# Short-convolution projections as 2x2x2 blocks in seven products, mixer outputs through DRAM scratch, two gates moved behind the last scan

## The chip, the core and the metric

One core of one Trainium2 chip runs the whole step. TensorE (PE, with its weight loads shown as PEld), VectorE (DVE), ScalarE (ACT), GpSimd (POOL) and the DMA queues work side by side, each in its own order; SyncE (SP) issues all transfers of this kernel. The metric is the device time of one execution in microseconds (us): three runs of the kernel before gave 1789.61, 1789.62 and 1792.41, median 1789.62.

## The reference

One layer of a hybrid decoder on 1088 tokens (1024 of a prompt, 64 of eight samples), width 1024, float32:

```python
h = rmsnorm(x, g_mix_pre) * (1 + scale_m) + shift_m
proj = h @ w_in                       # 1024 -> 3*1024 (B, C, x) + 1024 (z) + 2048 (xbc) + 16 (dt)
sc_b, sc_c, sc_x, z, xbc, dt_raw = jnp.split(proj, idx, axis=-1)
u = sc_c * sc_x
uc, new_sc_buf = causal_dwconv(u, sc_buf, sc_conv_w)
y_sc = sc_b * uc
xbc_c = silu(causal_dwconv(xbc, ...))                 # x, B, C of the scan, 4 groups
y_ssd, new_state = ssd_scan(xs, dt, A, Bm, Cm, d_skip, ssm_state)
yg = (y_ssd * silu(z)).reshape(bsz, L, SSM_GROUPS, SSM_WIDTH // SSM_GROUPS)
y_ssd = rmsnorm(yg, 1.0).reshape(bsz, L, SSM_WIDTH) * ssm_norm_g
mix = jnp.concatenate([y_sc, y_ssd], axis=-1) @ w_out
x = x + gate_m * rmsnorm(mix, g_mix_post)
f = (silu(h2 @ w_gate) * (h2 @ w_up)) @ w_down        # h2: normed and modulated x
x = x + gate_f * rmsnorm(f, g_ffn_post)
```

The modulation vectors (shift, scale, gate) are six slices of silu(c) @ w_ada + b_ada. The outputs are x, the new convolution rows and the new scan states.

## The kernel before

Activations lie transposed: 128 channels on the partitions, 1088 tokens along the row. Every large product takes float32 operands as a high part `hi` (a cast on ACT) and a rest `lo` (a subtraction on DVE), and is three matmuls per 128 input channels: `hi*hi`, `hi*lo`, `lo*hi` (`acc3`, lines 335 to 340). The modulated input is held as eight pairs `hh[k]`, `hl[k]`.

A planner orders the instructions. It goes by program order, takes what is ready by its own estimate of times, and writes out one fixed order for each engine; a tile has a slot in a pool with a fixed number of buffers, and its first writer waits until a slot is free. `in_order` (line 1073) puts the PE instructions of a call behind the last PE instruction traced before it, and only those.

The stages, in order:

- the input norm, the modulation and the first projection (lines 94 to 567);
- four scan groups, `ssd(g)` (line 693). `merge` (line 955) interleaves its steps with a list `side` that gives PE other work: `group_tiles(g+1)` (the projections of the next group), from g=1 on `gate(g-1)` (line 892: six projection tiles of z, silu, multiply) and `norm(g-1)` (line 903: squares, column sums on PE, a chain of small DVE operations for the inverse root, `rsqrt_of`, line 263, its spread over the partitions on PE, `spread`, line 276, and the scaling), and at g=3 `short_conv(0)`;
- `gate(3)`, then `short_conv(1)` to `short_conv(3)` (line 914), into which `norm(3)` and the two later modulation products `ada_steps(1)`, `ada_steps(2)` (line 188) are merged. A call of `short_conv` covers 256 channels: C, x and B, each two output tiles of three token chunks (`CH`: 384, 384, 320 columns) with 24 matmuls; u = C*x, a convolution over three rows and the multiply by B follow on DVE;
- the output projection (lines 1042 to 1165): first the scan half, whose eight outputs are split into hi and lo from where they stand (lines 1057 to 1063), for all tokens; then the short-convolution half in three token chunks, split by `out_split` (line 1078), with the residual rows of the chunk before (`mix_tail`, line 1113) between its tiles;
- the feed-forward part (lines 1167 to the end). Its gate and up products are already 2x2x2 blocks in seven products: `combos_w` (line 1258) builds seven weight combinations from two raw halves, `sums_x` (line 1240) four sums of the input blocks, and `unit` (line 1313) runs the seven products in the order of `ORDER` (line 1174) for two token blocks `QS` of halves of 256 and 288 columns: 7 * 2 * 4 * 3 = 168 matmuls for 256 output channels, into PSUM banks A, C and B; after each product the running sum is copied (ACT) or added (DVE) to its output.

```python
    ORDER = ((1, "A", True, 0, 0, True), (5, "C", True, 1, 1, True), (6, "A", False, 0, 1, True),
             (3, "C", False, 0, 1, False), (7, "A", False, 1, 1, False), (2, "B", True, 0, 0, False),
             (4, "A", False, 1, 0, True))
```

(each entry: product, bank, whether the bank is new, output block, half, whether it is that output's first write)

The mixer's outputs stay on chip, most of them in the 18 buffers of the pool `fmp`, until the output projection has read them.

## Time and profile before

| what | us |
|---|---|
| median of three runs | 1789.62 |
| the profiled execution | 1787.29 |
| its span, first to last instruction | 1785.6 |
| PE busy in the span | 1715.8 |
| DVE busy in the span | 1066.7 |
| four scan groups (125 to 545 us of the span) | 420 |
| gate(3), short_conv(1..3), two modulation products (545 to 800) | 255 |
| output projection and residual (800 to 1060) | 260 |

The profile's page gives busy time per engine, the span in 40 slices, the DMA queues, the chain of work that ended last and the costliest groups. In a group's row stand the line, engine, operation, tiles (out<-in), shapes, count, then busy us and the mean ns of one, then the idle time of the engine just before them with what ended it. A matmul's mean is longer than its spacing, since matmuls overlap; the spacing is a stretch of time divided by the number of matmuls in it. The view of stretches gives, for each, its length, then busy us and instruction count of each engine, the granted PE clock, the DMA share and GB/s. The timeline gives start, duration, engine, line and operation, with runs of the same instruction merged.

### The profile page before, as it was taken

The numbers are of one execution on the slowest core, as the hardware profiler recorded it, in microseconds if no ns is written. First come the engines' busy times: TensorE is split into PE (matmuls) and PEld (weight loads), VectorE is DVE, ScalarE is ACT, GpSimd is POOL, SyncE is SP. The second block draws the span as 40 slices with busy tenths as digits, with TensorE's granted clock in tenths as the row PEclk, the third lists the DMA queues.
The fourth block names the chain that finished last, engine by engine and source line by source line (L and its number), as shares of the span: only waits on it lengthen the run. The fifth ranks groups of instructions, "written<-read, shape, count | busy, mean of one in ns | idle before, by whom it ended". The sixth has DMA issues, their size and how long they took to land.

```text
span 1785.6 us, 30704 instructions
## 1 busy us (share of the span) xinstructions
PE 1715.8 (96%) x12336; PEld 1629.9 (91%) x12336; DVE 1066.7 (60%) x2175; ACT 716.1 (40%) x1485; POOL 261.3 (15%) x361
## 2 busy tenths in 40 slices
PE   5999999999999999999999899999999999899997
PEld 4998999998889999999989799999999998899987
DVE  5588777876562413142047868666665676678845
ACT  3456563554312110113245765444444444422303
POOL 2111001010010001000040000022222200332303
PEclk8999999999999999999999899999999999999999
DMA  9210303021112144432134833433434448856243
GB/s 313 72 35 25 86 13 100 22 70 42 35 58 64 60 140 151 144 104 90 48 101 147 259 116 124 144 136 136 147 134 150 152 156 293 329 208 243 101 150 119
DMA packets 144885, 224.02 MB, mean 125 GB/s; under 512 B 9153, under 2 KB 118897, under 8 KB 142438
## 3 DMA queue, kind: packets, MB, share of 16 engines
q1 hardware_dynamic: 144742, 222.06, 36.7%
q8 instruction: 97, 1.59, 0.4%
q14 instruction: 46, 0.38, 0.1%
HBM read 168.48 MB, written 53.55 MB: 124 GB/s over the span
## 4 chain that ended last, share of the span: by engine, by line
PE 84%; DVE 6%; ACT 3%; DMA 3%; issue 2%; POOL 1%; SPq 1%; DVEq 0%; POOLq 0%; ACTq 0%
PE pm L338 15%; PE pm L340 15%; PE pm L339 15%; PE pz L1309 5%; PE pz L1311 5%; PE pz L1310 5%; PE pm L1309 4%; PE pm L1311 4%; PE pm L1310 4%; PE pm L197 1%; PE pz L755 1%; DMA raw<-in_w_up 1%; PE pz L760 1%; DMA raw<-in_w_in 1%; PE pz L749 1%
## 5 line engine op out<-in xcount | busy, mean ns | idle before, releaser
L340 PE MATMUL pm<-h,wl 128*128 128x384 f32 (+1 forms) x810 | 266.8, 329 | 0.0
L339 PE MATMUL pm<-h,wh 128*128 128x384 f32 (+1 forms) x810 | 266.7, 329 | 0.0
L338 PE MATMUL pm<-h,wh 128*128 128x384 f32 (+1 forms) x810 | 266.6, 329 | 0.0
L315 ACT CAST wh<-raw 128x512 fp32r<-128x512 f32 (+1 forms) x141 | 87.9, 651 | 312.3 <-PE pm L339 204.0
L316 DVE TENSOR_TENSOR wl<-raw,wh 128x512 fp32r<-128x512 f32 (+1 forms) x123 | 87.4, 726 | 146.6 <-ACT wh L315 143.1
L338 PEld LDWEIGHTS pm<-h,wh 128*128 128x128 f32 x810 | 153.0, 189 | 1.4 <-issue 1.0
L339 PEld LDWEIGHTS pm<-h,wh 128*128 128x128 f32 x810 | 152.9, 189 | 1.2 <-issue 0.7
L340 PEld LDWEIGHTS pm<-h,wl 128*128 128x128 f32 x810 | 152.9, 189 | 1.0 <-issue 0.9
L338 PE MATMUL pm<-bt,wh 128*128 128x384 f32 (+2 forms) x350 | 121.3, 347 | 0.5 <-ACT wh L315 0.5
L340 PE MATMUL pm<-bt,wl 128*128 128x384 f32 (+2 forms) x350 | 115.0, 329 | 0.2 <-DVE wl L316 0.2
L339 PE MATMUL pm<-bt,wh 128*128 128x384 f32 (+2 forms) x350 | 114.8, 328 | 0.0
L338 PEld LDWEIGHTS pm<-bt,wh 128*128 128x128 f32 x350 | 66.2, 189 | 18.4 <-issue 6.6
L432 DVE SCALAR_TENSOR_TENSOR fm<-ext,vT,fm 128x1024 f32<-128x1024 f32 x57 | 72.7, 1276 | 0.0
L1202 DVE TENSOR_TENSOR fs<-f,fs 128x512 fp32r<-128x512 f32 (+1 forms) x80 | 54.6, 695 | 26.9 <-ACT fs L1201 26.3
L339 PEld LDWEIGHTS pm<-bt,wh 128*128 128x128 f32 x350 | 66.4, 190 | 1.7 <-issue 0.3
L1201 ACT CAST fs<-f 128x512 fp32r<-128x512 f32 (+1 forms) x80 | 46.7, 598 | 52.7 <-DMA f_d<-fs 33.1
L340 PEld LDWEIGHTS pm<-bt,wl 128*128 128x128 f32 x350 | 66.3, 189 | 1.6 <-DVE wl L316 0.4
L1326 DVE TENSOR_TENSOR facc<-facc,pz 128x288 f32<-128x288 f32 x124 | 55.9, 451 | 15.8 <-PE pz L1311 15.5
L1326 DVE TENSOR_TENSOR facc<-facc,pm 128x256 f32<-128x256 f32 x124 | 51.5, 415 | 5.7 <-PE pm L1311 5.2
L1273 POOL TENSOR_TENSOR raw<-raw 128x512 f32<-128x512 f32 x16 | 22.1, 1378 | 206.4 <-DVE raw L1271 206.4
L338 PE MATMUL pm<-fm,wh 128*128 128x512 f32 (+2 forms) x144 | 46.6, 325 | 0.0
L340 PE MATMUL pm<-fm,wl 128*128 128x304 f32 (+2 forms) x144 | 46.6, 325 | 0.0
(4655 smaller groups left out, 5338.1 us busy)
## 6 DMA issues: line engine op xcount, KB each, us to landing
raw<-in_w_in SPq DMA_DIRECT2D x48, 512.0 KB
fc<-f_d SPq DMA_DIRECT2D x9, 2016.0 KB
f_d<-fs SPq DMA_DIRECT2D x31, 576.0 KB
wa<-in_w_ada SPq DMA_DIRECT2D x32, 512.0 KB
raw<-in_w_out SPq DMA_DIRECT2D x32, 512.0 KB
fc<-f_d SPq DMA_DIRECT2D x9, 1792.0 KB
f_d<-fs SPq DMA_DIRECT2D x31, 512.0 KB
raw<-in_w_gate SPq DMA_DIRECT2D x28, 512.0 KB
```

Source lines behind the costliest of these rows:

```text
L315: (nc.gpsimd.tensor_copy if hi_eng else nc.scalar.copy)(wh, raw)
L316: (eng or nc.vector).tensor_tensor(wl, raw, wh, op=sub)
L338: mm(ps[:, :n], wh, xh, start=(first and j == 0), stop=False)
L339: mm(ps[:, :n], wh, xl, start=False, stop=False)
L340: mm(ps[:, :n], wl, xh, start=False, stop=(last and j == end))
L432: nc.vector.scalar_tensor_tensor(po, e[:, j:j + NP], taps[j], po, op0=mult, op1=add)
L1201: nc.scalar.copy(hi, v)
L1202: (eng or nc.vector).tensor_tensor(lo, v, hi, op=sub)
L1309: mm(ps, W[0][k], X[0][k], start=(start and k == 0), stop=False, skip_group_check=True)
L1310: mm(ps, W[0][k], X[1][k], start=False, stop=False, skip_group_check=True)
L1311: mm(ps, W[1][k], X[0][k], start=False, stop=(stop and k == nk - 1), skip_group_check=True)
L1326: nc.vector.tensor_tensor(out(q, i, h), out(q, i, h), ps, op=add)
```

## The change

- **Short convolution.** The C, x and B projections of each 256 channels become three `unit`s (the function of the feed-forward part, with a new argument for the token blocks, here `SQ`: four halves of 272 columns). Their input blocks are `hh`/`hl` themselves for products 1 and 2, and sums of blocks for 5, 6, 4 (`sums_h`, into new tiles) and for 7 and 3; the sum for 7 is written over the second halves of `hh[0..3]`, `hl[0..3]` (`sums_last`), after the last plain projection has read them. All four channel groups now run after the last scan.
- **Order.** `ada_steps(1)` and `ada_steps(2)` move into the `side` of scan groups 1 and 2; `gate(0)`, `norm(0)` and `gate(1)` are the `side` of group 3; gates 2 and 3 run after it as `gate_late`, with the steps of `sums_h` and the first steps of `norm(1)` between their tiles; the rest of the norms 1, 2 and 3 is put between the products of the first two units (`late`), and what is left of them then runs ahead of the third.
- **norm.** It gets more steps (13), one chain of small operations for all nine token columns in place of three, the addition of squares on DVE in place of POOL, and ends by splitting its result and storing both parts in DRAM (`y_out`, scratch `y_d`). Its temporaries come from `new()`: a pool of one buffer (`psx`) for groups 1 to 3.
- **Outputs.** The short convolution's results are split and stored in the same way; the output projection loads hi and lo from `y_d` in both halves, and the splits there go.
- **gate.** silu is taken in place in PSUM (no `gz` tile).
- **Pools.** The scan groups' x tiles 2 to 7 lie in `yp2` (2 buffers) and `yp4` (4), which the units later use for C or x, for u (`e`) and for B (`cb`); `fmp` has 8 buffers. The feed-forward part is unchanged; its helpers stand earlier in the file.

```diff
+SQ = [(0, 272), (544, 272)]
...
+    h2p = pool(mid, "h2p", 4)
+    yp4, yp2 = pool(mid, "yp4", 4), pool(mid, "yp2", 2)
...
-        out = fm()
+        out = yt(yp2 if ct < 4 else yp4) if 1 < ct < 8 else fm()
...
+    def norm(g, y, new):
+        ps = pz()
+        sq = []
+        def sums(c):
+            for j in range(3):
+                mm(ps[:, 3 * c + j:3 * c + j + 1], sq[c][:, 0, j * P:(j + 1) * P], ones[:, 0:1],
+                   start=(c == 0 and j == 0), stop=(c == 2 and j == 2))
+        for c, (c0, n) in enumerate(CH):
+            q = new()[:, :768].rearrange("p (m n) -> p m n", m=2)
+            sq.append(q)
...
+            for m in range(2):
+                nc.scalar.square(q[:, m, :n], y[m][:, c0:c0 + n])
+            nc.vector.tensor_tensor(q[:, 0, :n], q[:, 0, :n], q[:, 1, :n], op=add)
+            yield
+            yield
+            sums(c)
+        r = rsqrt_of(ps[:, 0:9], 2 * P)
+        yield
+        yield
         for c, (c0, n) in enumerate(CH):
-            rs = spread(token_rstd(y, c), n)
+            rs = spread(r[:, 3 * c:3 * c + 3], n)
             for m in range(2):
                 v = y[m][:, c0:c0 + n]
                 nc.vector.scalar_tensor_tensor(v, v, sng[:, 2 * g + m:2 * g + m + 1], rs, op0=mult, op1=mult)
             yield
+        for m in range(2):
+            hi = new()[:, :T].bitcast(F32R)
+            lo = y[m].bitcast(F32R)
+            split(hi, lo, y[m])
+            y_out(8 + 2 * g + m, hi, lo)
+            yield
+
+    def y_out(k, hi, lo):
+        nc.sync.dma_start(y_d[k][:, 0], hi.bitcast(F32))
+        nc.sync.dma_start(y_d[k][:, 1], lo.bitcast(F32))
...
-        if g > 0:
-            side += [gate(g - 1, tl[g - 1][:2]), norm(g - 1, tl[g - 1][:2])]
+        side = [group_tiles(g + 1, tl[g + 1])] if g < 3 else []
+        if g in (1, 2):
+            side.append(ada_steps(g))
         if g == 3:
-            side.append(short_conv(0))
-        run(merge(ssd(g, *tl[g]), itertools.chain(*side), (0.67, 1.17, 1.17, 1.5)[g]))
-    ada = itertools.chain(ada_steps(1), ada_steps(2))
-    run(gate(3, tl[3][:2]))
-    run(merge(itertools.chain(short_conv(1), short_conv(2), short_conv(3)),
-              itertools.chain(norm(3, tl[3][:2]), ada), 0.4))
+            side += [gate(0, tl[0][:2]), norm(0, tl[0][:2], fm_row), gate(1, tl[1][:2])]
+        run(merge(ssd(g, *tl[g]), itertools.chain(*side), (0.67, 1.17, 1.17, 1.2)[g]))
...
+    left.close()
+    rws, wsc = pool(left, "rws", 4), pool(left, "wsc", 8)
+    x56, x4 = pool(left, "x56", 8), pool(left, "x4", 4)
+    pap, psx, psy = pool(left, "pap", 2), pool(left, "psx", 1), pool(left, "psy", 1)
...
+        vs_ = [pap, psx, pap]
+        for k in range(4):
+            v = [yt(in_turn(vs_)) for _ in range(2)]
+            for j in range(2):
+                nc.vector.tensor_tensor(v[j], hh[k + 4 * j], hl[k + 4 * j], op=add)
+            (b11, b12), (b21, b22) = blocks_h(v[0]), blocks_h(v[1])
+            nc.vector.tensor_tensor(b11, b12, b11, op=sub)
+            part(X_t[5][k][:, 0], X_t[5][k][:, 1], b11)
+            yield
...
+    def sums_last():
+        for k in range(4):
+            t = psy.tile([P, 2, 272], F32, tag="t3", name=nm("t3"))
...
+            nc.vector.tensor_tensor(t, b22l, b12l, op=sub)
+            nc.vector.tensor_tensor(t, t, b22h, op=add)
+            nc.vector.tensor_tensor(t, t, b12h, op=sub)
+            part(b12h, b12l, t)
...
+    sums = sums_h()
+    norm1, norm2, norm3 = (norm(g, ys[g], sx_row) for g in (1, 2, 3))
+    W2 = plain_w(w_in, 3072 + 512)
+    gate_late(2, ys[2], W2, {n: [sums, sums] for n in range(6)})
+    W3 = plain_w(w_in, 3072 + 768)
+    gate_late(3, ys[3], W3, {0: [norm1], 1: [norm1], 2: [norm1], 3: [norm1], 4: [norm1], 5: [norm1]})
+    run(sums)
+    sums_last()
...
+    late = [itertools.chain(norm1, norm2, norm3)]
+    pairs = [pap, yp2]
+    kept = []
+    for pr in range(4):
+        cc, cx = [[yt(pairs[(pr + j) % 2]) for _ in range(2)] for j in range(2)]
+        steps_ = {n: late for n in range(7)} if pr == 0 else {}
+        sc_unit(1024 + 256 * pr, cc, steps_)
+        sc_unit(2048 + 256 * pr, cx, steps_)
+        if pr == 0:
+            run(*late)
+        ext = []
+        for m in range(2):
...
+            e = yp4.tile([P, 1115], F32, tag="y", name=nm("y"))
...
+            conv(cc[m], e, es, [scw[:, j, ct:ct + 1] for j in range(3)], ct, None)
+            ext.append(e)
+        cb = [yt(yp4) for _ in range(2)]
+        sc_unit(256 * pr, cb, {})
+        for m in range(2):
+            y, hi, lo = cc[m], ext[m][:, :T].bitcast(F32R), cb[m].bitcast(F32R)
+            nc.vector.tensor_tensor(y, y, cb[m], op=mult)
+            split(hi, lo, y)
+            kept.append((2 * pr + m, hi, lo))
...
+    fa, fx, fb = pool(left, "fa", 4), pool(left, "fx", 8), pool(left, "fb", 7)
...
-    for k, y in enumerate(yall[8:]):
...
-        split(hi, lo, y)
+    for k in range(KT):
+        v = [(fx, btp, h2p)[(k > 3) + (k > 5)].tile([P, T], F32R, tag="bt" if k in (4, 5) else "fm", name=nm("hb"))
+             for _ in range(2)]
+        for e in range(2):
+            nc.sync.dma_start(v[e].bitcast(F32), y_d[8 + k][:, e])
...
-            split(*parts_, yall[k][:, c0:c0 + n])
+            nc.sync.dma_start(hb.bitcast(F32), y_d[k][:, :, c0:c0 + n])
...
-    out_proj(0, terms[0], {0: [nxt], 2: [nxt]}, lambda mp: out_load(mp, nc.gpsimd))
+    out_proj(0, terms[0], {0: [nxt], 2: [nxt]}, out_load)
```

`sc_unit` calls `unit` with the seven weight combinations of the given columns, all of them built on ACT and DVE; `late` is one list of one chain, so each product of the first two units takes one step of it.

More of the change, by code (lines that the diff above doesn't have):

```diff
@@ L141, in hymba_step @@
     load_first(1)
-    xt += [load_x(t, fmp, "fm") for t in range(3, 6)]
+    xt += [load_x(t, yp2 if t < 5 else yp4, "y") for t in range(3, 6)]
     wa0 += [load_quarter(q) for q in range(1, 4)]
@@ L146, in hymba_step @@
         hl.append(h_tile(k))
-    xt += [load_x(t, fmp, "fm") for t in range(6, 9)]
+    xt += [load_x(t, yp4, "y") for t in range(6, 9)]
     ident = const([P, P], "ident")
@@ new lines, in in_order, with in_turn, raw_half @@
+    def in_order(f, *a):
+        last = next(x for x in reversed(nc.cur_bb.bb.instructions) if x.engine == nc.tensor.engine)
+        with tc.issue_after(last):
+            return f(*a)
+    def in_turn(pools):
+        pools.append(pools.pop(0))
+        return pools[-1]
+    def raw_half(w, j, cols):
+        p = in_turn(raw_from)
+        raw = p.tile([P, 4, 256], F32, tag="bt" if p is btp else "wc", name=nm("raw"))
+        nc.sync.dma_start(raw, w[j * 512:(j + 1) * 512, cols:cols + 256].rearrange("(k p) n -> p k n", p=P))
+        return raw
@@ new lines, in plain_w, with product @@
+    def plain_w(w, cols):
+        raws = [raw_half(w, j, cols) for j in range(2)]
+        W = {}
+        for m in range(2):
+            for j in range(2):
+                t = in_turn(w_from).tile([P, 2, 4, P], F32R, tag="wc", name=nm("wp_"))
+                part(t[:, 0], t[:, 1], raws[j][:, :, m * P:(m + 1) * P])
+                W[m, j] = [[t[:, s, k] for k in range(4)] for s in range(2)]
+        return W
+    def product(ps, W, X, nk, start, stop):
+        for k in range(nk):
+            mm(ps, W[0][k], X[0][k], start=(start and k == 0), stop=False, skip_group_check=True)
+            mm(ps, W[0][k], X[1][k], start=False, stop=False, skip_group_check=True)
+            mm(ps, W[1][k], X[0][k], start=False, stop=(stop and k == nk - 1), skip_group_check=True)
@@ new lines, in unit @@
+    def unit(W, X, nk, qs, out, first=True, between={}, blocks_=QS):
+        B = {}
+        for n, (p, b, new, i, h, opens) in enumerate(ORDER):
+            for q in qs:
+                if new:
+                    B[b, q] = (pm, pz)[q]()
+                ps = B[b, q][:, :blocks_[q][1]]
+                in_order(product, ps, W[p], X[q][p], nk, new, p in (3, 2, 4))
+                if first and opens:
+                    nc.scalar.copy(out(q, i, h), ps)
+                else:
+                    nc.vector.tensor_tensor(out(q, i, h), out(q, i, h), ps, op=add)
+            for gen in between.get(n, ()):
+                in_order(next, gen, None)
@@ new lines, in sx_row, with sc_unit @@
+    def sx_row():
+        return yt(psx)
+    sums = sums_h()
[6 more added lines that the diff above has]
+    sums_last()
+    def sc_unit(cols, tiles, between):
+        unit(combos_w(w_in, cols, nc.vector), X_sc, 4, [0, 1],
+             lambda q, i, h: tiles[i][:, SQ[q][0] + 272 * h:SQ[q][0] + 272 * (h + 1)], True, between, SQ)
@@ L1149, in rows_fm @@
     def rows_fm():
[L1150 to L1152 removed]
+        return yt(yp4, (P, D))
+    G_m = post_rows(0, lambda: yt(yp2, (P, D)))
     terms = [out_split(0)]
```

266 lines of the change are left out of this document (108 added, 158 removed).

## The prediction

> **What bounds the kernel now.** I read the page first, for the busiest engine and the chain that ended last.
>
> ```profile
> span 1785.6 us, 30704 instructions
> PE 1715.8 (96%) x12336; PEld 1629.9 (91%) x12336; DVE 1066.7 (60%) x2175; ACT 716.1 (40%) x1485; POOL 261.3 (15%) x361
> PE 84%; DVE 6%; ACT 3%; DMA 3%; issue 2%; POOL 1%; SPq 1%; DVEq 0%; POOLq 0%; ACTq 0%
> ```
>
> PE is busy for 96% of the span and carries 84% of the chain. So a matmul less is time less, as long as nothing else becomes late. Then I read the view of stretches, one for each stage that the change touches.
>
> ```profile
> 552.00:572.00 20.00, 20.00 (x121) 20.00 (x120) 4.51 (x8) 6.51 (x15) 3.20 (x7) 1.00 0.16 53
> 1150.00:1450.00 300.00, 300.00 (x2391) 300.00 (x2390) 184.98 (x297) 141.64 (x284) 71.38 (x69) 1.00 0.40 142
> 125.00:205.00 80.00, 77.64 (x587) 68.92 (x586) 68.30 (x122) 48.80 (x105) 8.24 (x22) 1.00 0.25 69
> 409.00:545.00 136.00, 129.56 (x904) 121.28 (x903) 78.49 (x180) 43.32 (x101) 10.63 (x16) 0.97 0.17 50
> 545.00:800.00 255.00, 254.83 (x1574) 237.11 (x1573) 79.56 (x169) 36.82 (x71) 17.08 (x31) 1.00 0.34 110
> 900.00:1060.00 160.00, 146.46 (x977) 136.84 (x977) 103.99 (x219) 96.61 (x183) 23.38 (x25) 0.96 0.49 159
> ```
>
> The short convolution (545 to 800) leaves PE idle for 0.2 us of 255, with DVE at 31%: no latency shows there, and the stretch is pure matmul time. The scan groups are nearly as full, even group 0 (125 to 205), which has 46 us of projections beside it, 2.4 us idle of 80; group 3 (409 to 545) loses 6.4 us. So there is little idle time to win, and much to lose.
>
> **The products.** From 552 to 572 only plain projections run: 20 us / 121 = 165.3 ns per matmul, at a mean of 363 columns. From 1150 to 1450 only seven-product units run, with a mean of 272 columns: 300 / 2391 = 125.5 ns. A projection of 256 channels is now 144 matmuls, 23.8 us; a unit is 168, 21.1 us, 3.0 us a product. Twelve of them: 12 * 2.7 = **-32.6 us** (bounds -30 and -34, for a different split of columns). The weight combinations cost per unit what they cost there, and there PE stayed full with DVE at 62%, so I cost them at nothing for pairs 1 to 3.
>
> The Trainium skill, page "TensorE: Matmul & The Clock Gate", section "Back-to-back issue gap", speaks against this: it gives sustained spacings of about 81 ns at 128 columns and 131 ns at 512. On a straight line between them (an estimate from that page) 363 columns take 112 ns and 272 take 100, so that 168 matmuls would cost 0.7 us more than 144, and the twelve units +8 us in place of the gain. The two stretches of this trace disagree with it.
>
> **The late gates.** For what DVE and ACT must do beside gates 2, 3 and the first pair:
>
> ```profile
> L303 DVE TENSOR_TENSOR fm<-fm,fm 128x1088 fp32r<-128x1088 f32 x5 | 6.4, 1287 | 1.6 <-ACT fm L302 1.6
> L302 ACT CAST fm<-fm 128x1088 fp32r<-128x1088 f32 x6 | 6.6, 1097 | 1.9 <-DVE fm L303 1.9
> L1271 DVE TENSOR_TENSOR raw<-raw,raw 128x512 f32<-128x512 f32 x20 | 14.3, 716 | 0.6
> L1202 DVE TENSOR_TENSOR fs<-f,fs 128x512 fp32r<-128x512 f32 x27 | 19.7, 729 | 17.4 <-ACT fs L1201 17.1
> L898 DVE TENSOR_TENSOR fm<-fm,gz 128x384 f32<-128x384 f32 x7 | 3.9, 558 | 16.8 <-ACT gz L897 16.8
> L908 DVE SCALAR_TENSOR_TENSOR fm<-fm,vT,pz 128x384 f32<-128x384 f32 x10 | 5.7, 611 | 4.6 <-PE pz L279 4.6
> ```
>
> `sums_h` has 8 additions of whole rows (8 * 1.29 us) and 24 operations on 544 elements (24 * 0.77, the 512-element rows scaled): 28.7 us of DVE. The six tiles of gate 2 cover 144 * 0.165 = 23.8 us of it; some of the sums can start in the tail of group 3. The split of gate 3's weights stands behind them in program order, so gate 3 starts some 3 us late. `sums_last` can start only when gate 3's last tile has read `hh`: per k four DVE operations and a cast, with one temporary, 3.8 us, 15 us in all; product 7 needs it 12 us after the first unit starts. In the same stretch stands norm 1's chain of small operations; alone it takes what it takes now:
>
> ```profile
> 438.70 0.55 ACT L290 ACTIVATE gz<-fm 128x384 f32<-128x384 f32 x1
> 439.11 0.55 ACT L291 ACTIVATE gz<-fm 128x384 f32<-128x384 f32 x1
> 440.86 0.83 PE L294 MATMUL pz<-ones,gz 128*128 128x1 f32 x6 [0.38 <-POOL gz L292]
> 441.72 0.16 DVE L267 TENSOR_SCALAR sm<-pz 128x3 f32<-128x3 f32 x1 [2.07 <-PE pz L294]
> 444.94 0.16 DVE L273 SCALAR_TENSOR_TENSOR sm<-sm 128x3 f32<-128x3 f32 x1
> 445.24 0.91 PE L279 MATMUL pz<-ident,sm 128*128 128x128 f32 x6 [0.62 <-DVE sm L273]
> ```
>
> From 441.72 to 445.10 is 3.4 us. Its column sums end after the unit's first product, its spread is queued on PE behind the third, 6 us later, and everything after it on PE waits for it. Behind `sums_last` on DVE the chain ends some 11 us after the sums: PE waits about 5 us. Together **+8 us** (bounds 2, if the sums start early enough, and 20, if DVE, whose work from here to the end of pair 0 is about as long as PE's, falls further behind).
>
> **The rest of the norms.** Seven steps of norm 2 fall into the second unit, so the column sums of its last chunk are queued behind that unit's last product. All of what follows, the end of norm 2 and all of norm 3, runs ahead of the third unit, whose products are queued on PE behind norm 3's last spread. And everything goes through the single buffer of `psx`: norm 2's two `hi`, norm 3's three squares, norm 3's two `hi`; a `hi` gives the buffer back only when its store has landed. The nearest row for such a store is that of the feed-forward part, with two staging tiles:
>
> ```profile
> 1172.68 12.08 SPq L1374 DMA_DIRECT2D f_d<-fs  x6
>   DMA f_d<-fs: 26.1, 17
> ```
>
> Six stores of 0.5 MB in 12.08 us are three turns of each tile, so two turns in about 11, 5.5 us a turn, with a cast (0.65 us), a subtraction and waits in it; 17 casts waited for a store, 1.5 us each. I take 3.5 us for a store of 0.56 MB (bounds 2.5 and 4.5). Do buffers go out in program order, even where a later writer is ready sooner? SP's rows for one pool of four buffers:
>
> ```profile
> 63.86 0.39 SPq L307 DMA_DIRECT2D raw<-in_w_in  x1
> 87.82 0.39 SPq L833 DMA_DIRECT2D s<-in_state_ssm  x1
> 127.82 0.37 SPq L307 DMA_DIRECT2D raw<-in_w_in  x1
> 128.42 0.39 SPq L833 DMA_DIRECT2D s<-in_state_ssm  x1
> ```
>
> Weights and states alternate as the program has them, though the weight load at 127.8 had nothing to wait for but a buffer. I take program order. Counted from the end of the second unit: small operations 3.4, six scalings 3.6 (0.61 each) to 7.0; `hi` 1.1 + store 3.5, twice, to 16.2; three times two squares (0.96), an addition (0.56), three sums (0.42) and handovers (0.4) to 23.1; small operations and spread 3.9 to 27.0, where the third unit may start; scalings to 30.6; then `hi` 1.1, `lo` 1.3, store 3.5 to 36.5, and the second of the pair to 41. The unit's outputs `cb` go into `yp4`, whose buffers are held by these very tiles: bank A can't be copied out before 36.5, so product 6 starts at 36.9 and not at 6, product 3 at 41.5, and four products later, at 53.5, the unit ends; it would have ended at 21. That is **+32 us** (bounds 10, with fast stores and norm 3's squares taken ahead of norm 2's `hi`, and 36).
>
> An idle PE of this length has a price of its own in the clock column:
>
> ```profile
> 1000.00:1050.00 50.00, 41.34 (x316) 40.40 (x315) 37.23 (x95) 33.66 (x69) 0.11 (x1) 0.90 0.50 159
> ```
>
> 8.7 us idle go with a granted clock of 0.90: **+2 us** (0 to 5).
>
> **The output projection.** Its first half now loads 16 tiles of 0.56 MB, 8.9 MB; the fastest stretch of loads is
>
> ```profile
> 1500.00:1550.00 50.00, 43.62 (x290) 39.33 (x289) 29.09 (x81) 22.38 (x75) 12.60 (x23) 0.97 0.91 353
> ```
>
> At 353 GB/s that takes 25 us. The first buffers come free with products 5 and 6 of the last unit (15 and 12 us before its end), those on `hh` with product 7 (6 us before). The last tile lands some 11 us after the unit's end; the first output tile, 24 matmuls of 512 columns, 5.5 us by scaling the 165 ns, waits **+6 us** (2 to 12). What ACT and DVE no longer split hides behind PE in both kernels; the 13.5 us of idle PE from 900 to 1060 belong to the residual rows, which stay: 0 (-6 to 6).
>
> **The scan groups.** Groups 1 and 2 swap a gate (23.8 us) and a norm for a modulation product, which is all loads (8 MB) and little PE; group 3 keeps 47 us of its cover, as much as group 0 has with 2.4 us idle. Of group 3's 6.4 us, most goes with norm 2 and the short convolution. **-4 us** (-10 to +20: a modulation product late in group 1 or 2 covers less of the scan's tail and waits for loads).
>
> **Sum:** 1787.3 (the profiled execution; 1.7 outside its span, 2.3 under the median) - 32.6 + 8 + 32 + 2 + 6 - 4 = 1798.7; I say **1798**.
>
> **The rivals.**
> - *The norms are hidden* (faster). If buffers are given to whoever is ready, or the stores land in 2.5 us, the hole is 10 us in place of 32; with 5 us in the late gates, 4 for loads and clock and nothing from the scan groups that is 1787.3 - 32.6 + 10 + 5 + 4 = 1774. It turns at about 21 us of hole. For it: the planner fills PE's gaps at every other place (group 0); against it: the third unit's queue position is fixed and its output buffers are norm 3's.
> - *Half of it*: a hole of 20 us, the other terms as forecast: about 1787, no change that can be told.
> - *The scan starves* (slower still): the modulation loads stop PE in the tails of groups 1 and 2, +20 on the forecast: 1818. For it: 8 MB in a tail of some 30 us is 270 GB/s; against it: those loads had no wait in the row of 545 to 800.
> - *No gain in the products*: the units run no faster than 144 plain matmuls did, because the blocks' three pieces come from other tiles, or the spacing doesn't follow the columns: 1798 + 32.6 = 1831. The row of 1150 to 1450 speaks against it.
>
> **How the numbers follow.** Forecast 0.45 (1791 to 1810), hidden norms 0.34 (1762 to 1783), half 0.12, starving 0.07, no gain 0.02. A difference within 0.2%, 3.6 us, can't be told from none here. Faster: 0.34 and 0.02 of the half case, 0.36; same: the rest of that and the forecast's lower edge, 0.12; slower 0.52. The range leaves out the lower end of the hidden case (about 0.08) and the two slow rivals: 1765 to 1813; the likeliest case alone has 1791 to 1810.
>
> **What the profile after would show.** Right: units of pairs 1 to 3 at 125 ns with PE full; one gap of some 25 to 30 us between second and third unit of pair 0, ended by the small operations and the copies into `cb`; 4 to 8 us before the first output tile, ended by loads from scratch. Wrong: that gap under 15 us, units above 130 ns, or idle PE of more than 10 us in groups 1 and 2. The term I trust least is the hole: it is the planner's order, worked out by hand.

## The result, and the profile after

The changed kernel takes 1841.47 us, median of 4 runs (1835.78 to 1848.31), against 1790.03 us for the kernel before beside it: a ratio of 1.0286, 95% interval 1.0245 to 1.0328. It is slower, as the likeliest case had it, but by 51 us where that case had 8 to 11. The profiled execution took 1835.78 us, 48.5 more than that of before (1787.3). All stages below are from these two. One execution of the last experiment ran for 2741 us at a granted clock of 0.556; its ratio leaves it out.

The page's head and its chain, for the kernel after:

```profile
span 1834.1 us, 31585 instructions
PE 1710.3 (93%) x12624; PEld 1609.2 (88%) x12624; DVE 1172.7 (64%) x2263; ACT 775.5 (42%) x1595; POOL 234.1 (13%) x333
...
PE 79%; DVE 7%; DMA 6%; ACT 4%; issue 2%; POOL 1%; SPq 1%; DVEq 0%; POOLq 0%; ACTq 0%
```

PE has 5.5 us less busy time than before, in a span 48.5 us longer: it is idle for 123.8 us, where it was idle for 69.8. In the chain, PE fell from 84% to 79% and DMA rose from 3% to 6%. The view of stretches shows where. First before: scan groups 1 and 2, and the two halves of the output projection. The columns are the stretch, its length, the busy time of PE, PEld, DVE, ACT and POOL with their instructions, PE's granted clock, the DMA share and GB/s.

```profile
192.60:309.00 116.40, 115.42 (x839) 108.69 (x838) 85.27 (x173) 61.09 (x125) 13.19 (x28) 1.00 0.23 67
309.00:414.30 105.30, 104.33 (x766) 96.91 (x765) 80.71 (x168) 54.52 (x117) 12.16 (x22) 1.00 0.18 52
...
801.00:945.30 144.30, 144.12 (x823) 128.59 (x822) 41.18 (x59) 47.71 (x94) 21.39 (x17) 1.00 0.24 77
945.30:1100.20 154.90, 141.36 (x1083) 138.97 (x1081) 117.87 (x239) 100.36 (x182) 4.53 (x10) 0.96 0.52 171
```

After, the same stages, and between them the short convolution's twelve units in four stretches: the first unit, the second with the hole behind it, the third, and the other nine.

```profile
192.50:299.70 107.20, 95.95 (x654) 72.86 (x653) 68.53 (x120) 49.12 (x101) 12.02 (x23) 0.92 0.39 123
299.70:404.60 104.90, 93.41 (x653) 71.93 (x651) 64.59 (x115) 46.81 (x98) 13.61 (x21) 0.95 0.39 125
...
543.20:572.50 29.30, 25.40 (x193) 25.21 (x193) 23.01 (x49) 10.01 (x19) 0.00 (x0) 0.94 0.20 66
572.50:629.70 57.20, 35.11 (x242) 34.51 (x241) 36.10 (x77) 16.11 (x32) 4.15 (x11) 0.76 0.26 91
629.70:654.00 24.30, 21.74 (x171) 21.29 (x170) 14.36 (x22) 8.94 (x16) 0.00 (x0) 1.00 0.30 115
654.00:843.00 189.00, 189.00 (x1511) 189.00 (x1510) 125.83 (x202) 65.46 (x135) 9.58 (x25) 1.00 0.32 105
843.00:996.50 153.50, 147.28 (x822) 130.23 (x821) 32.22 (x47) 35.63 (x69) 0.00 (x0) 0.98 0.57 195
996.50:1149.60 153.10, 139.06 (x1083) 136.04 (x1081) 116.23 (x239) 100.36 (x182) 4.57 (x10) 0.97 0.48 159
```

Three things are to be seen. Nine units run with PE full: 189.0 us, 21.0 each, 125.1 ns per matmul. The second unit's stretch is 57.2 us long, and PE is busy for 35.1 us of it. And groups 1 and 2, which gave two gates away, are hardly shorter than before (212.1 us against 221.7), with PE idle for 22.7 us of them at a clock of 0.92 and 0.95.

The tails of the two groups, where no projection runs:

```profile
256.50:301.50 45.00, 33.75 (x226) 14.58 (x224) 24.87 (x46) 11.85 (x26) 8.76 (x8) 0.81 0.69 219
363.70:408.00 44.30, 32.81 (x225) 14.93 (x224) 26.62 (x49) 12.20 (x27) 9.11 (x8) 0.85 0.69 224
```

And what PE waited for in both groups (time in total, times, the longest):

```profile
PE pm L205 <- DMA wa<-in_w_ada: 12.9, 10, 4.5
```

And the row of the modulation products:

```profile
L205 PE MATMUL pm<-wa,cT 128*32 128x512 f32 x128 | 36.5, 738 | 13.0 <-DMA wa<-in_w_ada 12.9
```

The same products in the kernel before, by the view of groups (busy us, mean ns of one, idle time ahead of them):

```profile
L197 PE MATMUL pm<-wa,cT 128*32 128x512 f32 x128 | 17.1, 605 | 0.0
```

For 45 us in each group there are only the scan's own small matmuls and the modulation products, while DMA moves 219 and 224 GB/s. The products stop ten times for a load, and everything of the scan that is queued behind them on PE stops with them. The clock falls to 0.81 and 0.85: a modulation matmul, 605 ns before, took 738 ns on average. The next group's projections could run in such a tail. They don't come before 301.5, and SP's rows at the end of group 1 (start, length, issue) show why:

```profile
287.42 5.24 SPq L202 DMA_DIRECT2D wa<-in_w_ada  x2
...
293.64 0.93 SPq L299 DMA_DIRECT2D raw<-in_w_in  x2
```

Their weights (`raw`) go through the four buffers that the modulation's rows (`wa`) use, and are issued behind the last of these.

### The profile page after: what moved, and what is told of

Its sections match the earlier page's. It is cut to its first block, busy times and chain, and to the rows that moved or that the text cites. A ratio compares the mean times of both kernels' runs of the same rounds, so it can differ in the third digit from the quotient of the medians.

```text
span 1834.1 us, 31585 instructions
## 1 busy us (share of the span) xinstructions
PE 1710.3 (93%) x12624; PEld 1609.2 (88%) x12624; DVE 1172.7 (64%) x2263; ACT 775.5 (42%) x1595; POOL 234.1 (13%) x333
## 3 DMA queue, kind: packets, MB, share of 16 engines
q8 instruction: 99, 1.62, 0.4%
## 4 chain that ended last, share of the span: by engine, by line
PE 79%; DVE 7%; DMA 6%; ACT 4%; issue 2%; POOL 1%; SPq 1%; DVEq 0%; POOLq 0%; ACTq 0%
PE pm L330 9%; PE pm L332 9%; PE pm L331 9%; PE pz L1034 7%; PE pz L1036 7%; PE pz L1035 7%; PE pm L1034 7%; PE pm L1036 7%; PE pm L1035 7%; DMA wa<-in_w_ada 1%; DMA h<-in_w_ada 1%; PE pm L205 1%; DMA raw<-in_w_in 1%; PE pz L747 1%; PE pz L287 1%
## 5 line engine op out<-in xcount | busy, mean ns | idle before, releaser
L330 PE MATMUL pm<-hb,wh 128*128 128x512 f32 (+2 forms) x320 | 106.5, 338 | 6.2 <-ACT wh L307 6.2
L332 PE MATMUL pm<-hb,wl 128*128 128x512 f32 (+2 forms) x320 | 107.0, 337 | 1.9 <-DVE wl L308 1.9
L331 PE MATMUL pm<-hb,wh 128*128 128x512 f32 (+2 forms) x320 | 107.4, 337 | 0.0
L330 PE MATMUL pm<-h,wh 128*128 128x384 f32 (+1 forms) x306 | 101.9, 333 | 0.0
L331 PE MATMUL pm<-h,wh 128*128 128x384 f32 (+1 forms) x306 | 101.4, 331 | 0.0
L332 PE MATMUL pm<-h,wl 128*128 128x384 f32 (+1 forms) x306 | 101.3, 331 | 0.0
L330 PEld LDWEIGHTS pm<-hb,wh 128*128 128x128 f32 x320 | 60.7, 190 | 12.0 <-ACT wh L307 6.8
L332 PEld LDWEIGHTS pm<-hb,wl 128*128 128x128 f32 x320 | 60.5, 190 | 7.6 <-DVE wl L308 2.4
L331 PEld LDWEIGHTS pm<-hb,wh 128*128 128x128 f32 x320 | 60.9, 190 | 5.3
L330 PEld LDWEIGHTS pm<-h,wh 128*128 128x128 f32 x306 | 57.9, 189 | 1.6 <-issue 1.0
L332 PEld LDWEIGHTS pm<-h,wl 128*128 128x128 f32 x306 | 57.9, 189 | 0.8 <-issue 0.7
L331 PEld LDWEIGHTS pm<-h,wh 128*128 128x128 f32 x306 | 57.8, 189 | 0.8 <-issue 0.3
L205 PE MATMUL pm<-wa,cT 128*32 128x512 f32 x128 | 36.5, 738 | 13.0 <-DMA wa<-in_w_ada 12.9
L330 PE MATMUL pm<-bt,wh 128*128 128x384 f32 (+1 forms) x134 | 46.6, 348 | 0.0
L332 PE MATMUL pm<-bt,wl 128*128 128x384 f32 (+1 forms) x134 | 43.7, 326 | 0.2 <-DVE wl L308 0.2
```

The lines of the kernel that those rows point to most:

```text
L205: mm(ps[32 * j:32 * j + 32, :], cT[:, k, :], w[:, jj * 512:(jj + 1) * 512], start=(k == 0), stop=(k == KT - 1))
L330: mm(ps[:, :n], wh, xh, start=(first and j == 0), stop=False)
L331: mm(ps[:, :n], wh, xl, start=False, stop=False)
L332: mm(ps[:, :n], wl, xh, start=False, stop=(last and j == end))
```

## The experiments

The theory for the scan groups was that the modulation's loads, packed into the tails, stop PE; the rival was that the tails are the scan's own latency, laid bare. The theory for the hole was a chain of norm steps that is longer than the products beside it; its rivals were the single row buffer, and the third unit's wait for its buffers. Each edit is to the changed kernel unless another is named.

**e1, the modulation spread over the group**

```diff
-        if g in (1, 2):
-            side.append(ada_steps(g))
+        if g in (1, 2):
+            side = [alternate(side[0], ada_steps(g), (1, 1, 0))]
```

`alternate` takes one step of the first list, then as many of the second as the tuple says in turn.

> Only the order of the side list of scan groups 1 and 2 is changed: after every step of the group's projections comes a step of the modulation products (two in three), instead of all twelve projection steps first and the eight modulation steps behind them. The same work, the same loads. Theory (the tails of both groups stop on 8 MB of modulation rows that are all asked for in about 40 us, and have nothing else to do on TensorE): the waits of the modulation products on their loads fall from 12.9 us to under 4, groups 1 and 2 together fall from 212.1 us to about 184 to 192, and the whole time from 1841 to 1813 to 1822. Rival (the scan's own chain of small operations sets these stretches and the modulation products only fill holes in it): groups 1 and 2 stay within 5 us of 212 wherever the steps lie, the time stays at 1836 to 1848. Rival (the modulation's loads cost their bandwidth wherever they lie): the waits move from the tail to the projections' weights, groups 1 and 2 stay above 200.

1800.29 us (1797.03 to 1806.27; ratio to before 1.0059, interval 1.0037 to 1.0082): 41 us less than the changed kernel by the medians, 29.5 by the two profiled executions, which lie at opposite ends of their scatter. Groups 1 and 2 in the view of stretches:

```profile
197.50:285.00 87.50, 85.25 (x656) 70.92 (x655) 64.38 (x114) 44.29 (x96) 13.20 (x22) 1.00 0.47 146
285.00:376.00 91.00, 86.82 (x652) 71.93 (x649) 66.25 (x116) 44.17 (x96) 12.99 (x20) 0.98 0.47 143
```

PE's waits there (in total, times, the longest):

```profile
PE pm L205 <- DMA wa<-in_w_ada: 1.9, 1, 1.9
```

178.5 us in place of 212.1, with the same work: 33.6 us. The first theory stands, and both rivals fall. The gain is larger than expected: the stages are 5 us below the range given, the time 13 us below.

**e2, the modulation by itself, behind group 3**

```diff
-        if g in (1, 2):
-            side.append(ada_steps(g))
...
+    run(ada_steps(1), ada_steps(2))
     pre_scale("A_f", 4, gpre1)
```

> The modulation products are taken out of scan groups 1 and 2 and run by themselves behind group 3, so the tails of groups 1 and 2 keep neither projections nor modulation loads beside them. It measures what the scan's own tail takes bare, and what the modulation costs by itself. Theory (loads stop the tail): groups 1 and 2 together fall from 212.1 us to about 165 to 175 (184 less the modulation's 17.1 us of products and more), and the modulation alone takes some 30 to 40 us behind group 3, bound by its loads. Rival (the scan's own chain sets the tails): groups 1 and 2 stay above 200 us and the whole becomes longer by all that the modulation takes, 30 to 40 us.

1841.88 us, one run. Groups 1 and 2, and behind group 3 the modulation:

```profile
192.50:281.50 89.00, 87.33 (x654) 80.13 (x654) 69.97 (x123) 51.55 (x106) 10.00 (x24) 1.00 0.19 52
281.50:358.80 77.30, 75.48 (x579) 67.82 (x578) 62.27 (x110) 48.03 (x99) 10.09 (x17) 1.00 0.18 49
...
432.00:492.00 60.00, 36.55 (x140) 6.55 (x139) 3.95 (x7) 1.04 (x2) 4.93 (x4) 0.86 0.81 270
```

Groups 1 and 2 take 166.3 us, PE is idle for 3.5 us of them, and no pause between two projections is longer than 4.9 us: the next group's projections run where the tail was. So the tail isn't bare by itself, and the scan's latency is out as a cause. The theory had said that PE has nothing else to do there; it has, but the modulation stood ahead of it, on PE and in the load buffers. The modulation alone needs about 60 us for its 16.8 MB (270 GB/s at a DMA share of 0.81), 20 us or more above what was expected. Its PE time is 17.1 us, by the row of before. So groups 1 and 2 with their modulation ought to take 166.3 + 17.1 = 183 us at most (the matmul counts say that some 54 matmuls of group 3, about 9 us, lie in e2's two stretches); the changed kernel took 29 us more, and e1 took 178.5.

**e8, this part of the change alone, on the kernel before**

```diff
+        if g in (1, 2):
+            side.append(ada_steps(g))
-        run(merge(ssd(g, *tl[g]), itertools.chain(*side), (0.67, 1.17, 1.17, 1.5)[g]))
+        run(merge(ssd(g, *tl[g]), itertools.chain(*side), (0.67, 1.62, 1.62, 1.5)[g]))
...
-              itertools.chain(norm(3, tl[3][:2]), ada), 0.4))
+              itertools.chain(norm(3, tl[3][:2])), 0.4))
```

> The kernel before, with one part of the change alone: its sixteen modulation steps go from the short convolution's pairs 1 to 3 into scan groups 1 and 2, behind each group's projections, gate and norm. Theory (8 MB of rows asked for in the tail of a group cost the chip's DMA about 27 us, however much work stands ahead of them): the products wait 8 to 20 us on their loads in groups 1 and 2, which take 248 to 265 us where 221.7 and the 17.1 us of products would give 239; the pairs give back 17 us, and the time is 1797 to 1815. Rival (it was the gates' going that laid the tails bare, and the modulation only stood in them): with the gates still there the products do not wait, groups 1 and 2 take 236 to 242 us, and the time stays within 5 us of 1790.

1857.32 us (ratio 1.038, interval 1.036 to 1.0401): 67 us slower than before, far beyond what was expected. The tail of each group, from its last projection on:

```profile
284.00:344.00 60.00, 43.26 (x248) 23.09 (x247) 26.45 (x74) 11.16 (x22) 7.18 (x8) 0.63 0.53 167
...
433.00:490.00 57.00, 39.64 (x249) 21.55 (x248) 27.13 (x75) 11.78 (x23) 7.51 (x9) 0.71 0.61 185
```

PE's waits there (in total, times, the longest):

```profile
PE pm L197 <- DMA wa<-in_w_ada: 19.0, 7, 3.9
PE pz L279 <- DVE sm L273: 13.3, 6, 3.6
```

And the row of the modulation products:

```profile
L197 PE MATMUL pm<-wa,cT 128*32 128x512 f32 x128 | 36.7, 861 | 19.0 <-DMA wa<-in_w_ada 19.0
```

The gates are still there, and the tails are worse: 60 and 57 us at a clock of 0.63 and 0.71, with 19 us of waits for loads and 13 for the norm's roots, and modulation matmuls of 861 ns. The side list was also taken faster (1.62). The rival falls: with the gates kept, the block of loads at the end of the list still stops PE. How much of the 67 us is the block and how much the faster list, which uses up sooner what stands beside the scan, was not tried apart, and why this tail is longer than that of the changed kernel is not settled.

**e4, three norm steps per product**

```diff
-        steps_ = {n: late for n in range(7)} if pr == 0 else {}
+        steps_ = {n: 3 * late for n in range(7)} if pr == 0 else {}
```

> Three steps of the norms go behind each product of pair 0's first two units instead of one, so that none is left for the stretch ahead of its third unit; the row buffer stays one. Theory (the steps are a chain of about 86 us through one row buffer, against 42 us of products): the hole moves into the units, the three units of pair 0 together fall from 110.8 us by no more than 15, to 95 to 108, the time falls by 3 to 15 us. Rival (only the count of steps per product leaves the work over; the chain hides behind products once it is queued there): pair 0 falls to 68 to 80 us, the time by 30 us or more, to 1811 or less.

1838.30 us (ratio 1.0257, interval 1.0231 to 1.0283, which overlaps that of the changed kernel). Pair 0's three units took 108.6 us in place of 110.8. PE's waits there:

```profile
PE pz L905 <- DVE y L915: 13.8, 4, 6.1
PE pz L287 <- DVE sm L281: 9.4, 2, 8.5
```

In the changed kernel the same two waits are 14.0 us (3 times, the longest 10.9) and 12.0 us (3 times, 5.1). The hole is cut into pieces and is all there: the steps are a chain of some 86 us (543.2 to 629.7 in the changed kernel), and the 42 us of products in the first two units don't hide it in either queue order.

**e3, a second row buffer**

```diff
-    rws, wsc = pool(left, "rws", 4), pool(left, "wsc", 8)
+    rws, wsc = pool(left, "rws", 3), pool(left, "wsc", 8)
-    pap, psx, psy = pool(left, "pap", 2), pool(left, "psx", 1), pool(left, "psy", 1)
+    pap, psx, psy = pool(left, "pap", 2), pool(left, "psx", 2), pool(left, "psy", 1)
```

> The pool of one row that norms 2 and 3 use for squares and for the high parts (psx) gets a second buffer; to make room the raw weight tiles of the products go from four buffers to three. Theory (the hole of 35 us ahead of pair 0's third unit is the row buffer, held by each store for 2.8 us and by each square until its column sums are done): the stretch without products falls from about 36.5 us to 20 to 28, the time by 8 to 16 us to about 1827. Rival (the hole is the chain of norm 3 itself on VectorE and ScalarE, reciprocal roots included, and not the buffer): the stretch stays within 4 us of 36 and the time within 5 us of 1841.

1847.56 us (ratio 1.0315, interval 1.0299 to 1.033). The stretch without products went from 34.9 to 31.6 us, less than the theory's 8 to 16, so the buffer is a small part of the hole: PE's waits for squares fell from 14.0 to 7.8 us, but those for the roots rose from 12.0 to 14.2. As a verdict on the whole time the run is no use: the output projection now waited 17.6 us for a weight cast (6.2 before the edit), which may come from the raw tile that was given up, and groups 1 and 2, whose code is the same, took 218.7 us instead of 212.1.

**e5, the convolution states later** (on e1)

```diff
         if mp == 0:
             while kept:
                 y_out(*kept.pop(0))
+        if mp == 3:
             conv_state(ncs, 16, 3, o["ssmc_p"], o["ssmc_s"])
             conv_state(nsc, 8, 2, o["scc_p"], o["scc_s"])
```

What it is about is seen in SP's rows of the changed kernel, ahead of the load of the second column pair's weights:

```profile
851.83 0.32 SPq L1175 DMA_DIRECT2D out_ssmc_s<-y  x1
...
862.67 0.30 SPq L1175 DMA_DIRECT2D out_ssmc_s<-y  x1
...
871.60 0.32 SPq L1175 DMA_DIRECT2D out_scc_s<-y  x1
871.97 7.72 SPq L299 DMA_DIRECT2D raw<-in_w_out  x6
```

PE's waits there (in total, times, the longest):

```profile
PE pm L330 <- ACT wh L307: 6.2, 1, 6.2
```

The loads of the next weights are issued at 872, behind three pairs of stores of convolution states, each of which waits for a copy of something that PE transposes between its products; the load itself waits for nothing else that shows.

> The kernel with the modulation spread over groups 1 and 2 (e1_ada_spread), and in the output projection the convolution states' block is moved from behind the first column pair to behind the last one; the stores of pair 3's outputs stay where they were. Theory (the second column pair's raw weights are issued on SP behind the states' stores, which wait for ScalarE copies of transposes that TensorE does only behind 27 us of products; the wait of 6.2 us on the weight cast is that queue): the wait goes to under 1 us, the output projection's first half from 153.4 to 146 to 149, the time by 4 to 8 us below e1's 1800, to 1792 to 1797. Rival (the 17 MB of stores and loads through DRAM scratch hold the weights back by bandwidth alone): the wait stays at 4 us or more and the time within 2 us of e1's.

1797.44 us (ratio 1.0033, interval 1.002 to 1.0045), 2.9 under e1, with intervals that overlap. PE's wait is gone:

```profile
PE pm L330 <- ACT wh L307: 0.6, 1, 0.6
```

The queue is the cause of the wait. In the profile the output projection's first half takes 144.6 us (804.2 to 948.8), as long as in the kernel before (144.3), where e1 took 152.4 (811.3 to 963.7). That as much comes off the whole time is not shown.

**e6, the norms sooner** (on e1)

```diff
+        if g == 2:
+            side = [alternate(itertools.chain(side[0], gate(0, tl[0][:2])), ada_steps(2), (1, 0))]
+        if g == 3:
+            side = [alternate(gate(1, tl[1][:2]), norm(0, tl[0][:2], fm_row), (2,)), norm(1, tl[1][:2], fm_row)]
...
-    gate_late(3, ys[3], W3, {0: [norm1], 1: [norm1], 2: [norm1], 3: [norm1], 4: [norm1], 5: [norm1]})
+    gate_late(3, ys[3], W3, {n: [norm2, norm2] for n in range(6)})
...
-    late = [itertools.chain(norm1, norm2, norm3)]
+    late = [itertools.chain(norm2, norm3)]
```

Group 3's list is taken at 1.8 steps, and the second unit has two steps behind each of its first four products.

> On e1_ada_spread: gate 0 goes from group 3 to group 2, group 3 keeps gate 1 with norm 0 beside it and takes norm 1 behind it; the late gate 3 has two steps of norm 2 behind each chunk, and only norm 3 is left for pair 0's first two units. Nothing is left out. Theory (the hole of 35 us ahead of pair 0's third unit is two norms' chain through one row, 86 us for 33 steps, put behind 42 us of products): with 14 steps left the hole falls to 0 to 6 us, pair 0's three units from 110.8 us to 70 to 82; the time falls 25 to 38 us below e1's 1800, to 1762 to 1775. Rival (the hole is what the third unit waits for whatever the norms' count: DVE's convolution of pair 0 and the two buffers of yp4 it needs): pair 0 stays above 95 us, the time above 1785. Rival (the scan of group 3, with half of the gates gone from beside it, now stands bare): group 3 and the late gates grow by over 10 us from 133, and half of the gain is lost.

1804.08 us (ratio 1.0076, interval 1.0061 to 1.0091). Group 3's tail, and the first two units with most of the third:

```profile
437.00:490.00 53.00, 30.81 (x224) 25.46 (x222) 42.02 (x80) 19.57 (x39) 4.73 (x5) 0.65 0.36 126
...
543.40:614.60 71.20, 66.36 (x512) 65.65 (x511) 56.26 (x104) 28.50 (x56) 3.68 (x10) 0.95 0.29 100
```

Pair 0 took 76 us (its products end at 808.2, less nine units of 21.0, less the start at 543.4) against 110.8: the hole is gone, so it was the number of norm steps, and not the third unit's own buffers. Group 3's six gate chunks are used up at 437, and then come 53 us with PE idle for 22 at a clock of 0.65; from the group's start to the first unit it took 146.1 us, where e1 had 133.0 with six chunks (23.8 us) more in it. That is 37 us lost, all that the hole gave. The third rival, the bare scan, is one part of it; another is the longest wait there, for the late gate's first weights:

```profile
PE pm L330 <- ACT wp__625_4819 L1006: 13.2, 1, 13.2
```

**e7, gate 2 into group 3 as well** (on e6)

```diff
-            side = [alternate(gate(1, tl[1][:2]), norm(0, tl[0][:2], fm_row), (2,)), norm(1, tl[1][:2], fm_row)]
+            side = [alternate(itertools.chain(gate(1, tl[1][:2]), gate(2, tl[2][:2])),
+                              itertools.chain(norm(0, tl[0][:2], fm_row), norm(1, tl[1][:2], fm_row)), (2,))]
...
-    gate_late(2, ys[2], W2, {n: [sums, sums] for n in range(6)})
...
+    gate_late(3, ys[3], W3, {n: [sums, sums, norm2, norm2] for n in range(6)})
```

Group 3's list is taken at 2.15 steps, and the block sums take their temporaries from `pap` alone, so that `psx` is left to norm 2.

> As e6_norms_sooner, but gate 2 also goes into group 3 (gates 1 and 2 beside norms 0 and 1), so that one late gate of six chunks carries the block sums and norm 2 together. Theory: the projections are only moved, the norm chain is off the path as in e6, and group 3 keeps its cover of twelve chunks, so the time is within 8 us of e6's; if the sums (twelve steps of VectorE and ScalarE work) do not fit behind six chunks of 24 us, 5 to 15 us are lost ahead of the first unit, and the time is above e6's by that. Rival (the gate chunks beside the scan are what hides the scan): e7 is faster than e6 by over 10 us.

1791.91 us (ratio 1.001, interval 0.9997 to 1.0023), 12 us under e6: the rival is right that gate chunks beside the scan are what hides it. From group 3 to the first unit it took 133.2 us; the same 18 chunks took 146.1 in e6. Of these 12.9 us only 3.1 are idle time of PE; the rest is the same work done at a higher clock (0.92 over the stretch, 0.86 in e6). The wait for weights is left. PE's longest wait there (in total, times, the longest):

```profile
PE pm L330 <- ACT wp__637_4997 L1007: 14.3, 1, 14.3
```

The 14.3 us are the late gate's first weights. On SP their load stands behind the last stores of norm 1 and of the scan's states, and nothing was left on PE to run meanwhile.

**e9 and e10, chunks kept for that gap** (on e7, with e5's edit)

```diff
-                              itertools.chain(norm(0, tl[0][:2], fm_row), norm(1, tl[1][:2], fm_row)), (2,))]
-        run(merge(ssd(g, *tl[g]), itertools.chain(*side), (0.67, 1.17, 1.5, 2.15)[g]))
+                              itertools.chain(norm(0, tl[0][:2], fm_row), norm(1, tl[1][:2], fm_row)), 6 * (2,) + (4, 4, 4, 2, 0, 0))]
+        run(merge(ssd(g, *tl[g]), itertools.chain(*side), (0.67, 1.17, 1.5, 1.5)[g]))
```

e10 has 1.25 in place of the last 1.5.

> On e7_gate_sooner, with the convolution states' block moved as in e5_state_later. The side list of group 3 keeps its twelve gate chunks and norms 0 and 1, but the norms' steps are ordered so that they end before the last two chunks, and the list is taken more slowly (1.5 steps for each of the scan's instead of 2.15), so that about four gate chunks (16 us of products) are left behind the scan's last step. Nothing is left out. Theory (e7 waits 14.3 us on the late gate's first weight cast, because the weights' tiles lie where the scan's tiles lay and their loads stand on SP behind norm 1's stores; nothing is left on TensorE to cover that): the wait falls to under 4 us, the products between group 3's start and the first unit from 133 us to 118 to 124, and with e5's 4 to 8 us the time is 1768 to 1778. Rival (the late gate waits for the scan's last tiles, and these come later by as much as the chunks are put behind): the wait goes but group 3 grows by the same, and the time stays at 1784 or more.

> As e9_switch_covered, with the list taken more slowly still (1.25), which leaves about six of the twelve chunks behind the scan. Theory: the cover was enough in e9, so the time is within 4 us of it; if the scan with half the chunks beside it waits on itself, as group 3 of e6 did, the time is 5 to 15 us above e9's.

1777.06 us (ratio 0.9941, interval 0.9925 to 0.9956) and 1775.03 us (ratio 0.993, interval 0.9913 to 0.9947): both are faster than both kernels, by 0.6% to 0.7% of before, and the times lie where the theories had them. In e10, from group 3 to the first unit:

```profile
394.70:518.30 123.60, 113.87 (x835) 106.03 (x834) 104.76 (x209) 69.85 (x138) 4.78 (x6) 0.97 0.25 87
```

PE's waits from 394 to 592, which takes in the first two units (in total, times, the longest):

```profile
PE pz L287 <- DVE sm L281: 9.5, 2, 7.5
...
PE pm L330 <- ACT wp__637_4997 L1007: 1.0, 1, 1.0
```

The weights' wait went from 14.3 to 1.0 us and the stretch from 133.2 to 123.6 (127.5 in e9, short of what was expected there). What waits now in that stretch is the spread of norm 2, the 7.5 us.

**e11, norm 2's spread behind the first unit's first product** (on e10)

```diff
-    gate_late(3, ys[3], W3, {n: [sums, sums, norm2, norm2] for n in range(6)})
+    gate_late(3, ys[3], W3, {n: [sums, sums] + 2 * [norm2] * (n < 4) for n in range(6)})
...
-        steps_ = {n: late for n in range(7)} if pr == 0 else {}
+        steps_ = {n: (2 if n < 5 else 1) * late for n in range(7)} if pr == 0 else {}
```

> On e10_switch_covered_more: norm 2 gets two steps behind the first four chunks of the late gate only, so that the spread of its reciprocal roots stands behind the first unit's first product instead of behind the fifth chunk; the units take the steps left over, two behind most products. Theory (e10 waits 7.5 us on the spread because the eleven small VectorE operations of the root, 0.17 us each, take 10 us between the block sums' and the weights' operations, each of them 0.7 to 1.3 us): the longest wait falls to 0 to 3 us and the time by 3 to 8 us, to 1767 to 1772. Rival (VectorE is full in this stretch, and whatever is moved is late at the next place: the first unit's sums): the wait goes and the first unit grows by as much, the time within 2 us of 1775.

1777.75 us (ratio 0.9942, interval 0.9923 to 0.996), the same as e10. Group 3 to the first unit:

```profile
397.30:509.60 112.30, 110.09 (x818) 102.53 (x817) 93.59 (x188) 67.03 (x133) 4.78 (x6) 1.00 0.28 95
```

PE's longest wait behind it, up to 595 (in total, times, the longest):

```profile
PE pz L905 <- DVE y L915: 6.1, 1, 6.1
```

The stretch is 11 us shorter than in e10 and no wait in it is longer than 1.0 us, but pair 0, counted as in e6, took 90 us instead of 77: the rival. VectorE's chain is late at the next place.

## Why the prediction was wrong

The sign was right and the time was not; it lay 28 us above the range. By the prediction's terms, each measured against the same stage of before:

| term | forecast | measured | from |
|---|---|---|---|
| products | -32.6 | -33.6 | 12 * (23.8 - 21.0) |
| late gates | +8 | +8.3 | first unit 29.3, less 21.0 |
| hole, with its clock | +34 | +39.5 | second unit 57.2, third 24.3, less 21.0 each |
| output projection | +6 | +7.4 | 153.5 - 144.3, and 153.1 - 154.9 |
| scan groups, and all else from 192.5 to the first unit | -4 | +27.9 | 350.7 - (608.4 - 12 * 23.8) |
| sum | +11.4 | +49.5 | the profiled executions: +48.5 |

In the row of the scan groups, 350.7 us is the stretch from 192.5 to 543.2 in the changed kernel, and 608.4 that from 192.6 to 801.0 before, from which the twelve plain projections come off. By e2 groups 1 and 2 alone are 29 us over what they ought to take (212.1 against 183), so nearly all of the loss is theirs.

**The step that failed is "The scan groups", -4 us (-10 to +20).** It priced the modulation product as "all loads (8 MB) and little PE", and took from the short convolution of before that such loads have no wait. There they were spread over pairs 1 to 3, beside full projections. In the changed kernel the side list has all projections first and the modulation behind them, so that 8.4 MB come in one block, ahead of the next group's weights, and PE has 45 us in which nothing else is ready. The prediction had this mechanism among its rivals, with the sum "8 MB in a tail of some 30 us is 270 GB/s", at a price of 20 us and a chance of 0.07. e1 shows that the order alone makes 34 us; e2 shows that without these loads there is no tail, as the next group's projections fill it; e8 shows that such a block stops PE with the gates kept, too, though there the list was also taken faster. The bound of +20 saw a modulation product that is late and covers less; that the block also holds up the next group's projections, and lowers the clock of what runs between, was not in it. The prediction had named its own sign of being wrong here, more than 10 us of idle PE in groups 1 and 2; it was 22.7.

**The hole was right in place and kind, and 5 us too small, with larger errors inside it that partly cancel.** The rows of its first half, from the last column sums of norm 2 on:

```profile
594.93 0.72 PE L905 MATMUL pz<-ones,y 128*128 128x1 f32 x6
...
603.18 1.10 ACT L294 CAST y<-y 128x1088 fp32r<-128x1088 f32 x1 [7.15 <-DVE y L926]
604.31 0.34 SPq L936 DMA_DIRECT2D y_d<-y  x1
...
607.13 1.10 ACT L294 CAST y<-y 128x1088 fp32r<-128x1088 f32 x1 [2.85 <-DMA y_d<-y]
...
611.04 0.94 ACT L914 ACTIVATE y<-y 128x384 f32<-128x384 f32 x2 [2.81 <-DMA y_d<-y]
...
625.92 4.08 PE L287 MATMUL pz<-ident,sm 128*128 128x128 f32 x18 [5.11 <-DVE sm L281]
```

The store of `hi` gave the buffer back 2.8 us after its issue (forecast 3.5), so two of them took 7.9 us and not 9.2. The squares were slower: 611.0 to 620.8, 9.8 us for 6.9. And the root, from 620.84 to 625.8, took 5 us in place of 3.4, because VectorE did pair 0's convolution between its operations. Norm 3's spread began at 31.0 us and, with eighteen matmuls, took some 4, for which the forecast had half a microsecond: the third unit could start at 34.8 us in place of 27.0. On the other side, the third unit, which the forecast held up for 5.5 us until the buffers of `cb` came free, waited 2.6 us for them. That the hole is the number of steps is shown by e6, where 14 steps in place of 33 leave next to none, and by e4, where a denser queue brings nothing. The buffer, to which the prediction gave most room, is worth about 3 us by e3.

**The late gates** and **the output projection** came out near the forecast in size. Of the first unit's 8.3 us, 3.9 are the wait for norm 1's spread (forecast 5); the rest is busy time, the norm's own matmuls among it, at a clock of 0.94. Gate 3, which the forecast had start 3 us late, shows no wait. In the output projection the size was luck, since the cause was another: not the loads of the first tiles, which were in time, but the weights queued on SP behind the convolution states, as e5 shows, which gives back all of the first half's 9.2 us; a step that the change moves there, and for which the prediction had not counted the queue.

**The products** gave what was forecast, 125.1 ns in the units. By the line from the Trainium skill's page "TensorE: Matmul & The Clock Gate", section "Back-to-back issue gap", there would have been a loss of 8 us (the prediction's estimate); nine full units here speak against it.

Left open: how much of the tails' loss is bandwidth and how much is the four load buffers of 0.5 MB; a kernel with more of them was not tried. Nor was the scatter of the changed kernel's repeats, 12 us against 3 before, traced to a stage.

## What to carry to other kernels

Work that fills holes beside a chain should be spread along it by kind: a list that puts all the matrix work first and all the loads last stops the chain at its end, and holds back the next stage's loads, which would have covered it. When a faster product shortens the work that hid a chain of small operations, count the chain against what is left of the cover before counting the gain. And a block that is moved takes its stores with it: look at what is queued behind them on SP.

## What the hardware showed beyond that

A stalled PE was charged twice. In e8's tails a modulation matmul took 861 ns on average for 605 before, at a granted clock of 0.63 to 0.71. The Trainium skill, page "TensorE: Matmul & The Clock Gate", section "HAM oscillation — how this bites in real kernels", says that PE shouldn't stand idle for more than about 3.4 us at a time. The traces agree so far: PE's longest waits in e8's two tails were 3.6 and 3.9 us and in the changed kernel's 4.5 us, while e1's groups, with no wait above 2.2 us, had a clock of 1.00 and 0.98. No run tries the limit itself.

Small operations were as slow as the queue they stood in. In e10 the root of norm 2 is twelve VectorE operations of 0.17 us (the expectation said eleven); some of the rows (start, length, operation):

```profile
500.71 0.16 DVE L275 TENSOR_SCALAR sm<-pz 128x9 f32<-128x9 f32 x1
500.83 1.29 DVE L1093 TENSOR_TENSOR y<-h,h 128x1088 f32<-128x1088 f32 x1
...
502.68 0.17 DVE L276 TENSOR_SCALAR sm<-sm 128x9 int32<-128x9 int32 x1
...
510.84 0.16 DVE L281 SCALAR_TENSOR_TENSOR sm<-sm 128x9 f32<-128x9 f32 x1
```

Between them stand operations of 0.5 to 1.3 us of the block sums, the gates and the weights, so 2 us of work took 10.3, with VectorE busy for 9.7 of them. In the changed kernel, with a freer VectorE, norm 2's root took 2.9 us from its first to its last operation (595.69 to 598.59).
